# An encoder layer with a product-key expert FFN: chunk 0 routed before the last G, split weights for ten U blocks, one-hots moved to ScalarE, gathers spread later

## The chip, the cores and the metric

The kernel runs on one core of one Trainium2 chip. The metric is device time in microseconds, from one execution to the next of the same program; 0.5% of it is about 8 us. Five engines matter: TensorE (matmul, in the profile PE, its weight loads PEld), VectorE (DVE), ScalarE (ACT), GpSimd (POOL, here the queue of the gathers) and SyncE (SP, here the queue of all other loads and stores). Each works through its own list of instructions in order; semaphores tie the lists together.

## What is computed

One layer over 512 tokens of width 1024, in float32: two kinds of attention, a norm, and then the part that this case is about, a feed-forward layer with 16384 experts, each one row of a table U and one row of a table V. For each token, eight heads pick 16 experts each:

```python
q = (xb @ w_q).reshape(PEER_CHUNK, PEER_HEADS, PEER_KEY_DIM)
s1 = jnp.einsum('thd,kd->thk', q[..., :half], sub_keys[0])
s2 = jnp.einsum('thd,kd->thk', q[..., half:], sub_keys[1])
v1, i1 = lax.top_k(s1, PEER_TOPK)
v2, i2 = lax.top_k(s2, PEER_TOPK)
cand = (v1[..., :, None] + v2[..., None, :]).reshape(...)
cv, ci = lax.top_k(cand, PEER_TOPK)
...
idx = (e1 * PEER_N_KEYS + e2).reshape(PEER_CHUNK, PEER_HEADS * PEER_TOPK)
g = jax.nn.softmax(cv, axis=-1).reshape(PEER_CHUNK, -1)
hpre = jnp.einsum('td,ted->te', xb, u_table[idx])
act = g * jax.nn.gelu(hpre, approximate=False)
return jnp.einsum('te,ted->td', act, v_table[idx])
```

A gated term and the residual are added, and a last norm follows.

## The kernel before

The tokens are four chunks of 128. **Chunk 0 is gathered**: for each of its 128 slots, one indirect DMA fetches 128 rows of U (one per token, 512 KB), VectorE multiplies them with the tokens and sums; later the same with rows of V. **Chunks 1 to 3 are dense**: all 16384 experts are computed, in 128 blocks of 128. For the dense chunks the sparse weights g are spread into a matrix G (experts by tokens), which is written to DRAM and read back. The first 64 tokens of chunk 1 are mixed: their U products are gathered ("own rows", `own_rows`, 64 gathers of 128 rows, into the buffers `whi` and `wlo`), their V part is dense. So a U block covers N_U = 320 tokens, and an output block 384.

Matmuls at full precision are made of three at a reduced type: an operand is split into a high part (a cast on ScalarE, L78) and a low part (a subtraction on VectorE, L79), and `mm3` (L92 to L95) multiplies high x high, low x high, high x low. The `whole` form (L631) instead multiplies unsplit float32 weights with `whole`, a copy of the 320 tokens' h; it needs no cast, and each of its matmuls leaves two records in the trace. A matmul of the G step (L804), also float32, leaves two as well.

The work around the change, in order:

1. **Routing** (`route`, one call per chunk, four steps): VectorE alone, top-16 searches over candidate sums and lookups over 128 x 2048 tiles. For chunk 0 it ends in `i_sel`, the rows to gather.
2. **G** (`build_g`, one call per dense chunk): eight stages (each followed by a 1 MB store to `g_dram`), each of two steps of OT = 8 tokens. A step makes a first one-hot matrix for each token, `oh_i`: OV of the eight on VectorE in one instruction (L790), the others on ScalarE, one instruction each (L794), then one instruction over all of those (L795). VectorE makes the eight second ones (L799), TensorE multiplies eight pairs (L804), and ScalarE copies the result in two halves (L807) to the stage.
3. **Fill** (`filler`, advanced by `run_fill`): the gate product and then the first LEAD = 44 U blocks (`expert_in`), all in the whole form. A block is one 512 KB load, eight matmuls, one Gelu (L633). The Gelu of the first 16 blocks is stored in DRAM, of the others kept. `FILL_ROUTE` and `FILL_G` say how many fill steps are recorded per step of routing and stage of G, and `FILL_S` how many own rows.
4. The order is: routing of chunk 1; routing and G of chunk 2, then of chunk 3, with own rows and fill between; the G of chunk 1, whose weights include the own rows' results; routing of chunk 0; the rest of the fill. Then the memory of these stages (pool pR, which holds `whole` and the G buffers) is given up.
5. **The loop** over 128 blocks: as long as n + LEAD < 128 (84 turns) one more U block, in split form; then a V block is loaded and split, G is multiplied with the block's Gelu (L995), cast (`a_hi`) and subtracted (`a_lo`), and 18 output matmuls of 512 columns add into six accumulators. VectorE's order in the loop is written out by hand: each turn ends with some of the 257 gather steps of chunk 0 (L925 and L927 for U, L936 and L938 for V), which share four buffers `gat`. A turn with a U block counts 1, a later one 0.25, and the steps are spread evenly over that count:

```python
spent += 1 if n + LEAD < 128 else 0.25
upto = min(len(steps), math.ceil(len(steps) * spent / (128 - 0.75 * LEAD - 3)))
```

The loop's buffers lie where pool pR lay, so none of its loads can start before pR's tiles are done. Buffers named `raw` (three), `whi` and `wlo` (two each) serve all split weights before and in the loop, and psH two accumulators for U blocks. Outside the loop a scheduler sets the order within each engine from the order in which the steps were recorded.

Of the kernel before, what the change touches and what calls it, by code (L numbers as in the profile page):

```python
# [33 lines left out]
GB = 8  # L34
LEAD = 44
SPILL = 16
FILL_ROUTE = 1.7
FILL_G = 1.0
FILL_S = 2.8
OT = 8  # L40
OV = 5
NEG = -1e30
NA_KEYS = 256
NA_FROM = (0, 64, 192, 256)
# [10 lines left out]
def tile_encoder_layer(ctx: ExitStack, tc: tile.TileContext, A: dict, out: bass.AP):  # L55
# [550 lines left out]
    NGC, NDC = N_G // 128, N_D // 128  # L606
# [12 lines left out]
    def expert_in(i, whole=None):  # L619


        ps = psH.tile([128, 512], F32, name="hp")
        if whole is None:
            u = stream(A["uT"][i], [8, 128])
            for k in range(8):
                mm3(ps[:, :N_U], (u[0][:, k], u[1][:, k]), (hTh[:, k, ts], hTl[:, k, ts]), k == 0, k == 7)
        else:
            u = wst.tile([128, 8, 128], F32, name="raw", bufs=3)
            nc.sync.dma_start(u, A["uT"][i])
            for k in range(8):  # L630
                nc.tensor.matmul(ps[:, :N_U], u[:, k], whole[:, k, :], start=(k == 0), stop=(k == 7))  # L631
# [143 lines left out]
    def build_g(c, e1, e2, gw):  # L775
# [8 lines left out]
        for tg in range(128 // GT):  # L784
            stage = rt.tile([128, 128, GT], F32, name="g_st", bufs=2)
            for q in range(GT // OT):
# [5 lines left out]
                                        op=OP.is_equal)  # L792
                for i in range(OV, OT):
                    nc.scalar.activation(oi[:, i], iota, AF.Abs, bias=ne[:, t0 + i:t0 + i + 1])  # L794
# [22 lines left out]
    whole = rg.tile([128, 8, N_U], F32, name="whole")  # L817
# [25 lines left out]
    def filler():  # L843
        blocks = iter(range(LEAD))
        for hf in range(2):
            hs = slice(hf * 512, (hf + 1) * 512)
            gps = [ps_tile("mm", 4) for _ in range(4)]
            for kk in range(4):
                w = stream(A["gate_w"][kk * 256:(kk + 1) * 256, hs].rearrange("(k p) n -> p k n", p=128), [2, 512])
                for k2 in range(2):  # L850
                    k = 2 * kk + k2
                    for c in range(4):
                        cs = slice(c * 128, (c + 1) * 128)
                        mm3(gps[c], (hTh[:, k, cs], hTl[:, k, cs]), (w[0][:, k2], w[1][:, k2]), k == 0, k == 7)
                yield

            for c in range(4):
                pl = rg.tile([128, 512], F32, name="pl", bufs=2)
                nc.sync.dma_start(pl, ple_dram[c, :, hs])
                z = gps[c]  # L860
                nc.vector.tensor_tensor(z, z, gb[:, hs], op=OP.add)
                nc.scalar.activation(z, z, AF.Tanh, scale=0.5)
                nc.vector.scalar_tensor_tensor(z, z, 1.0, pl, op0=OP.add, op1=OP.mult)
                nc.vector.scalar_tensor_tensor(base[c][:, hs], h[c][:, hs], ALPHA, z, op0=OP.mult, op1=OP.add)
                if c % 2:
                    expert_in(next(blocks), whole)
                    yield
        for i in blocks:
            expert_in(i, whole)
            yield  # L870

    fill = filler()
    due = 2.0

    def run_fill(amount):
        nonlocal due
        due += amount
        while due >= 1:
            next(fill, None)
            due -= 1  # L880

    run_fill(0)
    gathers, g_due = iter(()), 0.0

    def run_own(amount):
        nonlocal g_due
        g_due += amount
        while g_due >= 1:
            next(gathers, None)
            g_due -= 1  # L890

    held = []
    for c in list(range(NGC, 4)):
        res = []
        for _ in route(c, res):
            run_fill(FILL_ROUTE)
            run_own(FILL_S)
        if c == NGC:
            held = res
            gathers = own_rows(*res)  # L900
            continue
        for _ in build_g(c, *res):
            run_fill(FILL_G)
            run_own(FILL_S)
    for _ in gathers:
        pass
    for _ in build_g(NGC, *held):
        run_fill(FILL_G)
    for c in range(NGC):
        for _ in route(c, []):  # L910
            run_fill(FILL_ROUTE)
    for _ in fill:
        pass
    pR.close()
# [52 lines left out]
    with tc.manual_schedule(engines={nc.vector.engine}):  # L967
        for n, i in enumerate(order):
            if n + LEAD < 128:
                expert_in(n + LEAD)  # L970
            if n % GB == 0:
                gt = gt_next
            if n % GB == GB // 2 and n + GB // 2 < 128:
                gt_next = load_g(n + GB // 2)
            raw = pE.tile([128, D], F32, name="v_raw", bufs=3)
            nc.sync.dma_start(raw, v_rows[i * 128:(i + 1) * 128, :])
            if n in (124, 125):
                vh = wst.tile([128, D], F32R, name="whi")
                vl = wst.tile([128, D], F32R, name="wlo")
                a2 = wst.tile([128, 2, N_D], F32R, name="raw", bufs=3)  # L980
                ah, al = a2[:, 0], a2[:, 1]
            else:
                vh = pE.tile([128, D], F32R, name="v_hi")
                vl = pE.tile([128, D], F32R, name="v_lo")
                ah = pE.tile([128, N_D], F32R, name="a_hi")
                al = pE.tile([128, N_D], F32R, name="a_lo")
            split(vh, vl, raw)
            if i < SPILL:
                ge = pE.tile([128, N_U], F32, name="ge_in", bufs=2)
                nc.sync.dma_start(ge, ge_dram[i])  # L990
# [121 lines left out]
```

## Time and profile before

| | |
|---|---|
| median of three runs | 1638.03 us (1636.96 to 1643.42) |
| the profiled execution | 1644.48 us, span 1642.7 us |
| TensorE busy | 1564.1 us, 95% of the span |
| VectorE busy | 1328.0 us, 81% |
| ScalarE busy | 671.3 us, 41% |
| GpSimd busy | 553.3 us, 34% |
| DMA | 409.13 MB, mean 249 GB/s |

The page of the profile shows shares of the whole span, groups of equal instructions with their mean time and with the idle time of the engine ahead of them, and the chain of waits from the end back to the start. Here the stages differ much, so they are read one by one: a table of busy time by stretch, then the timeline of single engines. In a timeline row stand start, length, engine, line, instruction, output and inputs, count, and in brackets the idle time ahead of it with what ended it. Line numbers are those of the kernel before.

### The profile page before, as it was taken

The numbers are of one execution on the slowest core, as the hardware profiler recorded it, in microseconds if no ns is written. First come the engines' busy times: TensorE is split into PE (matmuls) and PEld (weight loads), VectorE is DVE, ScalarE is ACT, GpSimd is POOL, SyncE is SP. The second block draws the span as 40 slices with busy tenths as digits, with TensorE's granted clock in tenths as the row PEclk, the third lists the DMA queues.
The fourth block names the chain that finished last, engine by engine and source line by source line (L and its number), as shares of the span: only waits on it lengthen the run. The fifth ranks groups of instructions, "written<-read, shape, count | busy, mean of one in ns | idle before, by whom it ended". The sixth has DMA issues, their size and how long they took to land.

```text
span 1642.7 us, 23609 instructions
## 1 busy us (share of the span) xinstructions
PE 1564.1 (95%) x8195; PEld 1309.7 (80%) x8195; DVE 1328.0 (81%) x2959; ACT 671.3 (41%) x1190; POOL 553.3 (34%) x407
## 2 busy tenths in 40 slices
PE   6999899999999999996899999999999999999997
PEld 4788677888777767784788888888898888888885
DVE  7366794699999999995778888878888888877776
ACT  3356684433324626682333333333343333333343
POOL 1013100000114453200455555555455565543200
PEclk9999999999999999998899999999999999999999
DMA  7242340332469988756899999999999999987763
GB/s 223 61 127 75 86 124 14 119 90 78 118 219 318 373 320 301 288 226 233 309 340 323 359 325 350 361 323 336 354 324 334 358 327 350 344 291 257 260 237 110
DMA packets 190583, 409.13 MB, mean 249 GB/s; under 512 B 14592, under 2 KB 100992, under 8 KB 187392
## 3 DMA queue, kind: packets, MB, share of 16 engines
q1 hardware_dynamic: 141696, 234.06, 41.9%
q0 software_dynamic: 48768, 173.56, 29.3%
q8 instruction: 65, 1.06, 0.3%
q14 instruction: 54, 0.44, 0.1%
HBM read 372.64 MB, written 31.98 MB: 246 GB/s over the span
## 4 chain that ended last, share of the span: by engine, by line
PE 40%; DMA 22%; issue 15%; DVE 14%; POOL 7%; ACT 2%; SPq 1%; DVEq 0%; POOLq 0%; ACTq 0%
DMA gat<-in_u_rows_dram,i_sel 11%; DMA gat<-in_v_rows_dram,i_sel 8%; PE hp L631 4%; PE acc L93 4%; PE acc L95 4%; PE acc L94 4%; POOL gat L925 3%; PE tr L804 3%; PE pj L93 3%; PE mm L93 3%; PE pj L94 3%; PE pj L95 3%; PE mm L94 3%; PE mm L95 3%; POOL gat L936 3%
## 5 line engine op out<-in xcount | busy, mean ns | idle before, releaser
L93 PE MATMUL acc<-v_hi,a_hi 128*128 128x512 f32 x756 | 297.6, 394 | 14.2 <-ACT a_hi L78 14.2
L95 PE MATMUL acc<-v_hi,a_lo 128*128 128x512 f32 x756 | 296.8, 393 | 0.0
L94 PE MATMUL acc<-v_lo,a_hi 128*128 128x512 f32 x756 | 294.9, 390 | 0.0
L925 POOL DMA_INDIRECT gat<-in_u_rows_dram,i_sel x128 | 203.2, 1588 | 260.2 <-DVE scr L927 147.8
L936 POOL DMA_INDIRECT gat<-in_v_rows_dram,i_sel x128 | 210.6, 1646 | 202.7 <-DVE base L938 172.6
L78 ACT CAST a_hi<-gt 128x384 fp32r<-128x384 f32 x126 | 64.9, 515 | 478.7 <-DVE gt L995 476.5
L95 PE MATMUL hp<-hTh,wlo 128*128 128x320 f32 x672 | 211.2, 314 | 17.9 <-DVE wlo L79 17.5
L93 PE MATMUL hp<-hTh,whi 128*128 128x320 f32 x672 | 208.7, 311 | 1.0 <-ACT ge L633 1.0
L94 PE MATMUL hp<-hTl,whi 128*128 128x320 f32 x672 | 208.2, 310 | 0.0
L631 PE MATMUL hp<-whole,raw 128*128 128x320 f32 x704 | 200.3, 433 | 0.0
L78 ACT CAST whi<-raw 128x1024 fp32r<-128x1024 f32 (+3 forms) x137 | 138.4, 1010 | 131.2 <-PE mm L94 53.1
L79 DVE TENSOR_TENSOR wlo<-raw,whi 128x1024 fp32r<-128x1024 f32 (+3 forms) x137 | 159.8, 1167 | 37.7 <-ACT whi L78 37.3
L79 DVE TENSOR_TENSOR v_lo<-v_raw,v_hi 128x1024 fp32r<-128x1024 f32 x126 | 153.7, 1220 | 39.4 <-DMA v_raw<-in_v_rows_dram 19.6
L927 DVE SCALAR_TENSOR_TENSOR scr<-gat,h 128x1024 f32<-128x1024 f32 x128 | 156.5, 1223 | 35.5 <-DMA gat<-in_u_rows_dram,i_sel 33.7
L938 DVE SCALAR_TENSOR_TENSOR base<-gat,hdot,base 128x1024 f32<-128x1024 f32 x128 | 164.1, 1282 | 21.6 <-DMA gat<-in_v_rows_dram,i_sel 20.1
L93 PEld LDWEIGHTS acc<-v_hi,a_hi 128*128 128x128 f32 x756 | 142.3, 188 | 41.9 <-ACT a_hi L78 15.4
L95 PEld LDWEIGHTS acc<-v_hi,a_lo 128*128 128x128 f32 x756 | 142.3, 188 | 33.7 <-DVE a_lo L79 1.4
L631 PEld LDWEIGHTS hp<-whole,raw 128*128 128x128 f32 x704 | 128.9, 190 | 45.6
L94 PEld LDWEIGHTS acc<-v_lo,a_hi 128*128 128x128 f32 x756 | 142.5, 188 | 27.6
L78 ACT CAST v_hi<-v_raw 128x1024 fp32r<-128x1024 f32 x126 | 131.9, 1047 | 54.6 <-PE acc L95 33.4
L95 PEld LDWEIGHTS hp<-hTh,wlo 128*128 128x128 f32 x672 | 127.3, 189 | 26.0 <-DVE wlo L79 25.9
L79 DVE TENSOR_TENSOR a_lo<-gt,a_hi 128x384 fp32r<-128x384 f32 x126 | 70.4, 559 | 80.4 <-ACT a_hi L78 79.1
(343 smaller groups left out, 2863.9 us busy)
## 6 DMA issues: line engine op xcount, KB each, us to landing
raw<-in_uT_dram SPq DMA_DIRECT2D x128, 512.0 KB
v_raw<-in_v_rows_dram SPq DMA_DIRECT2D x128, 512.0 KB
g_dram<-g_st SPq DMA_DIRECT2D x24, 1024.0 KB
gt<-g_dram SPq DMA_DIRECT2D x16, 1536.0 KB
raw<-in_w_in_dram SPq DMA_DIRECT2D x17, 512.0 KB
raw<-in_w_q_dram SPq DMA_DIRECT2D x16, 512.0 KB
na_b<-in_na_bias_dram POOLq DMA_DIRECT2D x32, 128.0 KB
raw<-in_w_o_dram SPq DMA_DIRECT2D x8, 512.0 KB
```

Source lines behind the costliest of these rows:

```text
L78: nc.scalar.copy(hi, src)
L79: nc.vector.tensor_tensor(lo, src, r32(hi), op=OP.subtract)
L93: nc.tensor.matmul(ps, a[0], b[0], start=start, stop=False)
L94: nc.tensor.matmul(ps, a[0], b[1], start=False, stop=False)
L95: nc.tensor.matmul(ps, a[1], b[0], start=False, stop=stop)
L631: nc.tensor.matmul(ps[:, :N_U], u[:, k], whole[:, k, :], start=(k == 0), stop=(k == 7))
L804: nc.tensor.matmul(ps[:, i * 128:(i + 1) * 128], oj[:, 4 * r + i, :], oi[:, 4 * r + i, :], start=True, stop=True)
L925: nc.gpsimd.indirect_dma_start(out=u[:], out_offset=None, in_=u_rows, in_offset=bass.IndirectOffsetOnAxis(ap=i_sel[:, c, k:k + 1], axis=0))
L927: nc.vector.scalar_tensor_tensor(scr, u, 1.0, h[c], op0=OP.mult, op1=OP.mult, accum_out=hdot[:, c, k:k + 1])
L936: nc.gpsimd.indirect_dma_start(out=u[:], out_offset=None, in_=v_rows, in_offset=bass.IndirectOffsetOnAxis(ap=i_sel[:, c, k:k + 1], axis=0))
L938: nc.vector.scalar_tensor_tensor(base[c], u, hdot[:, c, k:k + 1], base[c], op0=OP.mult, op1=OP.add)
```

## The change

Six numbers and the order of the stages change. The numbers of instructions that differ are: 80 fewer `whole` matmuls (ten blocks), 240 more split ones, ten more casts each on ScalarE and VectorE, 144 more L794, L795 over 768 elements instead of 384, and L790 over 256 instead of 640. GpSimd's list is the same.

```diff
-FILL_ROUTE = 1.7
-FILL_G = 1.0
-FILL_S = 2.8
+SPLIT_LEAD = 10
+FILL_ROUTE = 1.3
+FILL_G = 0.35
+FILL_OWN = 0.7
+OWN = 2.8
+LATE_GATHER = 0.4
 OT = 8
-OV = 5
+OV = 2
...
         for i in blocks:
-            expert_in(i, whole)
+            expert_in(i, whole if i < LEAD - SPLIT_LEAD else None)
             yield
...
-    held = []
-    for c in list(range(NGC, 4)):
-        res = []
-        for _ in route(c, res):
-            run_fill(FILL_ROUTE)
-            run_own(FILL_S)
-        if c == NGC:
-            held = res
-            gathers = own_rows(*res)
-            continue
-        for _ in build_g(c, *res):
-            run_fill(FILL_G)
-            run_own(FILL_S)
-    for _ in gathers:
+    def paced(steps, rate, own=None):
+
+        due = 0.0
+        for _ in steps:
+            due += OWN if own is not None else 0
+            while due >= 1:
+                next(own, None)
+                due -= 1
+            run_fill(rate + (FILL_OWN if own is not None else 0))
+
+    held = []
+    paced(route(NGC, held), FILL_ROUTE)
+    own = own_rows(*held)
+    for c in range(NGC + 1, 4):
+        res = []
+        paced(route(c, res), FILL_ROUTE, own)
+        paced(build_g(c, *res), FILL_G, own)
+    for _ in own:
         pass
-    for _ in build_g(NGC, *held):
-        run_fill(FILL_G)
     for c in range(NGC):
-        for _ in route(c, []):
-            run_fill(FILL_ROUTE)
+        paced(route(c, []), FILL_ROUTE)
+    paced(build_g(NGC, *held), FILL_G)
     for _ in fill:
         pass
...
-            spent += 1 if n + LEAD < 128 else 0.25
-            upto = min(len(steps), math.ceil(len(steps) * spent / (128 - 0.75 * LEAD - 3)))
+            spent += 1 if n + LEAD < 128 else LATE_GATHER
+            upto = min(len(steps), math.ceil(len(steps) * spent / (128 - (1 - LATE_GATHER) * LEAD - 3)))
```

So chunk 0's routing comes before the G of chunk 1 instead of after it; the last ten of the 44 U blocks done ahead no longer read `whole`; two of eight first one-hots stay on VectorE; fewer fill steps are recorded beside a stage of G without own rows, and about as many as before beside one with them (0.35 + 0.7); and a turn of the loop without a U block counts 0.4 in the spread of the gathers.

More of the change, by code (lines that the diff above doesn't have):

```diff
@@ L882, in tile_encoder_layer @@
     run_fill(0)
[L883 to L890, printed above, removed]
+    def paced(steps, rate, own=None):
[6 more added lines that the diff above has]
+            run_fill(rate + (FILL_OWN if own is not None else 0))
     held = []
-    for c in list(range(NGC, 4)):
+    paced(route(NGC, held), FILL_ROUTE)
+    own = own_rows(*held)
+    for c in range(NGC + 1, 4):
         res = []
-        for _ in route(c, res):
-            run_fill(FILL_ROUTE)
-            run_own(FILL_S)
-        if c == NGC:
-            held = res
-            gathers = own_rows(*res)
-            continue
-        for _ in build_g(c, *res):
-            run_fill(FILL_G)
-            run_own(FILL_S)
-    for _ in gathers:
-        pass
-    for _ in build_g(NGC, *held):
-        run_fill(FILL_G)
+        paced(route(c, res), FILL_ROUTE, own)
+        paced(build_g(c, *res), FILL_G, own)
+    for _ in own:
+        pass
     for c in range(NGC):
-        for _ in route(c, []):
-            run_fill(FILL_ROUTE)
+        paced(route(c, []), FILL_ROUTE)
+    paced(build_g(NGC, *held), FILL_G)
     for _ in fill:
```

## The prediction

> **What bounds the kernel now.** I read the table by stage first, because the share of the whole span (TensorE 95%) averages stages with different limits. The stages are cut where the trace changes: routing and the G of chunks 2 and 3 (440 to 690), the G of chunk 1 (690 to 737), routing of chunk 0 (737 to 762), a hole, the loop with U blocks (782 to 1451) and the loop without (to 1622). Columns: stage, length, then busy us and instructions of TensorE, weight loads, VectorE, ScalarE, GpSimd; granted clock, DMA share, GB/s.
>
> ```profile
> 440.00:690.00 250.00, 240.77 (x1182) 183.91 (x1181) 242.84 (x648) 110.59 (x247) 93.21 (x64) 1.00 0.82 297
> 512.00:586.00 74.00, 73.03 (x411) 58.01 (x411) 72.49 (x200) 44.44 (x107) 30.30 (x23) 1.00 0.94 346
> 622.00:690.00 68.00, 67.00 (x385) 53.83 (x384) 66.89 (x185) 43.23 (x106) 21.61 (x16) 1.00 0.84 307
> 690.00:737.00 47.00, 47.00 (x325) 40.90 (x324) 46.97 (x162) 40.73 (x101) 0.00 (x0) 1.00 0.58 223
> 737.00:762.00 25.00, 25.00 (x95) 17.64 (x95) 22.96 (x79) 6.89 (x11) 0.00 (x0) 1.00 0.44 159
> 762.00:782.00 20.00, 4.79 (x31) 4.19 (x29) 1.66 (x3) 5.09 (x7) 3.78 (x4) 0.68 0.85 304
> 782.00:1451.00 669.00, 651.12 (x3499) 579.39 (x3500) 557.18 (x698) 227.63 (x331) 376.61 (x234) 0.99 0.95 338
> 1451.00:1622.00 171.00, 170.94 (x749) 139.10 (x748) 124.39 (x163) 69.44 (x90) 33.47 (x19) 1.00 0.71 247
> ```
>
> Up to 737 VectorE is never free (242.84 of 250, 46.97 of 47). ScalarE is half idle while chunks 2 and 3 get their G, but not in the G of chunk 1: 40.73 of 47. From 762 to 782 nearly everything stands still, and the clock falls to 0.68. The next rows (timeline: start, length, instruction, idle before it and its releaser) show that hole and TensorE's pace around it.
>
> ```profile
> 736.94 25.47 PE L631 MATMUL hp<-whole,raw 128*128 128x320 f32 x94
> 762.48 0.38 SPq L962 DMA_DIRECT2D gt<-g_dram  x1
> 779.76 1.23 DVE L79 TENSOR_TENSOR v_lo<-v_raw,v_hi 128x1024 fp32r<-128x1024 f32 x1 [19.56 <-DMA v_raw<-in_v_rows_dram]
> 781.99 0.79 PE L93 MATMUL acc<-v_hi,a_hi 128*128 128x512 f32 x1 [14.17 <-ACT a_hi L78]
> 788.13 0.31 PE L95 MATMUL hp<-hTh,wlo 128*128 128x320 f32 x1
> 791.36 0.40 PE L93 MATMUL acc<-v_hi,a_hi 128*128 128x512 f32 x1
> 795.26 0.39 PE L95 MATMUL acc<-v_hi,a_lo 128*128 128x512 f32 x1
> ```
>
> The first loads of the loop leave only at 762.48, when the last whole-weight block, and with it the memory of the G stage, is done. VectorE then waits 19.56 us for a V block. A whole block costs 25.47 / 94 x 16 = 4.34 us of TensorE (16 records each). Split matmuls follow each other at (791.36 - 788.13) / 22 = 0.147 us, so a split block of 24 takes 3.52; an output matmul takes (795.26 - 791.36) / 17 = 0.229, 18 of them 4.13. A turn of the loop with a U block is thus 7.65 us of TensorE, but 84 turns took 669, 7.96 each. VectorE's groups in 782 to 1451 say why (last columns: idle ahead of the group, and what ended it), and so do four starts of the same instruction in successive turns:
>
> ```profile
> L927 DVE SCALAR_TENSOR_TENSOR scr<-gat,h 128x1024 f32<-128x1024 f32 x128 | 156.5, 1223 | 35.5 <-DMA gat<-in_u_rows_dram,i_sel 33.7
> L938 DVE SCALAR_TENSOR_TENSOR base<-gat,hdot,base 128x1024 f32<-128x1024 f32 x106 | 136.0, 1283 | 21.6 <-DMA gat<-in_v_rows_dram,i_sel 20.1
> L79 DVE TENSOR_TENSOR a_lo<-gt,a_hi 128x384 fp32r<-128x384 f32 x84 | 46.9, 559 | 54.6 <-ACT a_hi L78 53.3 <-issue 1.3
> 1001.43 0.56 DVE L79 TENSOR_TENSOR a_lo<-gt,a_hi 128x384 fp32r<-128x384 f32 x1 [0.64 <-ACT a_hi L78]
> 1008.98 0.56 DVE L79 TENSOR_TENSOR a_lo<-gt,a_hi 128x384 fp32r<-128x384 f32 x1 [0.64 <-ACT a_hi L78]
> 1017.18 0.56 DVE L79 TENSOR_TENSOR a_lo<-gt,a_hi 128x384 fp32r<-128x384 f32 x1 [0.64 <-ACT a_hi L78]
> 1023.46 0.56 DVE L79 TENSOR_TENSOR a_lo<-gt,a_hi 128x384 fp32r<-128x384 f32 x1 [0.64 <-ACT a_hi L78]
> ```
>
> A turn with three gathers keeps VectorE 7.55 us (1001.43 to 1008.98) if no gather is late, one with two 6.28 (1017.18 to 1023.46). 257 steps over 92 units are 2.79 a turn, 7.28 us; the waits for gathers, 33.7 + 20.1 = 53.8 us, add 0.64: 7.92. So VectorE, in its written order, sets the turn, and late gathers push it past TensorE.
>
> **The loop with fewer gathers a turn.** The new spread divides by 128 - 0.6 x 44 - 3 = 98.6: 2.61 steps a turn, in the order 3, 3, 2, 3, 2. VectorE's own work is then (3 x 7.55 + 2 x 6.28) / 5 = 7.04. Even with the old wait of 0.64 it asks for 7.68, about TensorE's 7.65. DMA does not forbid it: 338 GB/s over 7.96 us is 2.69 MB a turn, less 0.18 of a 0.52 MB gather is 2.60, at 338 GB/s 7.69 us. But 651.12 us of busy TensorE over 84 turns is 7.75, and I take that: 84 x (7.96 - 7.75) = -18 us. Ends: -27 (7.65) and -8 (7.87, half of the waits stay).
>
> The gathers put off go to the 44 later turns, 1.04 a turn instead of 0.7. There a gather in each turn makes VectorE's chain as long as the output matmuls:
>
> ```profile
> 1504.14 0.56 DVE L79 TENSOR_TENSOR a_lo<-gt,a_hi 128x384 fp32r<-128x384 f32 x1 [0.64 <-ACT a_hi L78]
> 1508.50 0.56 DVE L79 TENSOR_TENSOR a_lo<-gt,a_hi 128x384 fp32r<-128x384 f32 x1 [0.92 <-ACT a_hi L78]
> ```
>
> This pair is 4.36 us apart, TensorE's turn 4.13. Over 36 turns that is at most 36 x 0.23 = 8 us, at least nothing; most of it hides behind the two buffers ahead of TensorE, so +3. The last gather comes four turns later, some eight turns before the end, and the norm of chunk 0 still fits there.
>
> **Six of eight one-hots on ScalarE.** Groups in 690 to 737, the G of chunk 1, of 16 steps of eight tokens; then one step on each engine; then a wide cast, for the price of width.
>
> ```profile
> L807 ACT COPY g_st<-tr 128x512 f32<-128x512 f32 x32 | 18.7, 583 | 5.5 <-PE tr L804 5.4
> L794 ACT ACTIVATE oh_i<-iota,ne 128x128 f32<-128x128 f32 x48 | 15.9, 397 | 0.0
> L795 ACT ACTIVATE oh_i<-oh_i 128x384 f32<-128x384 f32 x16 | 8.4, 526 | 0.2
> L790 DVE TENSOR_TENSOR oh_i<-iota,eT 128x640 f32<-128x640 f32 x16 | 12.9, 808 | 0.0
> 697.47 0.81 DVE L790 TENSOR_TENSOR oh_i<-iota,eT 128x640 f32<-128x640 f32 x1
> 700.25 0.81 DVE L790 TENSOR_TENSOR oh_i<-iota,eT 128x640 f32<-128x640 f32 x1
> 704.65 1.95 PE L804 MATMUL tr<-oh_i,oh_j 128*128 128x128 f32 x16
> 705.28 0.53 ACT L795 ACTIVATE oh_i<-oh_i 128x384 f32<-128x384 f32 x1
> 705.74 0.59 ACT L807 COPY g_st<-tr 128x512 f32<-128x512 f32 x1
> 706.63 0.59 ACT L807 COPY g_st<-tr 128x512 f32<-128x512 f32 x1 [0.31 <-PE tr L804]
> L78 ACT CAST v_hi<-v_raw 128x1024 fp32r<-128x1024 f32 x126 | 131.9, 1047 | 54.6 <-PE acc L95 33.4
> ```
>
> A step is 2.78 us of VectorE now (697.47 to 700.25). 256 elements instead of 640 cut it by 0.40 to 0.48 (0.808 x 384 / 640 at most; some of an instruction does not scale). ScalarE's step grows: three more L794 at 15.9 / 48 = 0.33 are 1.0; L795 over 768 lies between 526 and 1047 ns, 0.84, 0.31 more. Its 40.73 / 16 = 2.55 becomes 3.8 if it never waits. In its written order (three L794, copy, one, copy, two, L795) each first copy also waits for half of the eight matmuls that L795 released, 1 us of the 1.95 above, while three L794 cover only 0.9 of that and of the hand-overs: 0.3 to 0.4 a step, as in the row at 706.63. I take 4.1 us, ScalarE now setting the pace. The G of chunk 1 goes from 46 to 16 x 4.1 + 1 = 67: +21. Ends: 3.6 (the rows' starts are closer than their lengths, 0.46 of 0.53) gives +13, 4.4 gives +25.
>
> For chunks 2 and 3, where own rows are dotted between the steps, a step is 74 / 16 = 4.6 and 68 / 16 = 4.25 us. VectorE falls by 0.4 to 4.1 and 3.8, ScalarE rises by 1.3 to 4.1 and 4.0 before any wait, and DMA is at 0.94 and 0.84. Three limits lie within 0.5 us, so I take 0. Ends: -13 (32 x 0.4, all of VectorE's cut is gained) and +10 (0.3 a step lost to ScalarE's order).
>
> **The reordered stage and the split weights.** In the built programs 34.5 whole blocks stand ahead of chunk 1's G before; after it is 30 ahead of chunk 0's routing. In that routing come four whole and three split blocks, 4 x 4.34 + 3 x 3.52 = 28 us of TensorE, beside 23 us of routing and 5 casts of 1.2 on VectorE: also 28. The fifth cast waits for a buffer that the third split block frees, and chunk 1's one-hots stand behind it on VectorE, and behind that block's Gelu on ScalarE, so they start after all 28. Two split blocks fit into the G, and 142 matmuls x 0.147 = 21 us follow it; the last G store, the G load and V blocks run under them. The hole took 19.5 us from load to first output matmul, a store now comes first, so I add 2: 23. SP's stores of that G stand behind the eighth split load, which waits only for the fifth cast; GpSimd's order does not change. Sum from 690: 28 + 67 + 23 = 118 us against 92 (690 to 782), +26, of which +21 is the line above and +5 this. If the loads were not covered, the hole would be 20 again: ends +3 and +15.
>
> **Sum:** +5 (order) + 21 (G of chunk 1) + 0 (G of chunks 2, 3) - 18 (loop) + 3 (late turns) = +11. The profiled execution took 1644.48 us (span 1642.7), 6.4 above the median of the three runs, so 1655.5 in its own terms is 1649 against 1638.03.
>
> **The rivals.**
> *ScalarE doesn't set the pace (faster).* If its step is 3.6, since its rows overlap, the G of chunk 1 costs +13, and chunks 2 and 3 follow VectorE, -13. Then +5 + 13 - 13 - 18 + 3 = -10: 1628. It decides from a step under about 3.9. For it: VectorE is at 98% in 440 to 690, ScalarE at 44%. Against it: 40.73 of 47 already, and DMA at 0.94.
> *The parts cancel.* The loop falls to 7.65, all 54 us of waits hidden: -27, and +5 + 21 + 0 - 27 + 3 = +2: 1640. For it: 2.61 steps ask VectorE for only 7.04. Against it: 7.75 of TensorE is busy in a turn.
> *TensorE cools in the G of chunk 1.* It works 1.95 us and waits 2.1, sixteen times. If the clock is halved there, as it nearly was in the hole (0.68), its 1.95 becomes 3.9, both copies wait longer, and a step is about 5.8: 16 x 1.7 = +27 more, 1676. Against it: the clock fell only where TensorE stood for 14 us. The Trainium skill, "TensorE: Matmul & The Clock Gate", section "A second HAM failure mode: psum-queue depth-cycling", speaks for it: frequent short idling between groups of matmuls makes the clock swing between half and full; no run here shows it yet.
>
> **How the numbers follow.** Forecast 0.45 (its own range 1640 to 1662), ScalarE not the limit 0.27, cancelling 0.20, cooling 0.08. The measurement can tell 0.5%, 8 us, from no change. The forecast is slower by more than that in most of its range, and some of it reaches into the middle: slower 0.50, same 0.21, faster 0.29. The range takes in the faster case with a larger gain in the loop and most of the cooling: 1621 to 1671.
>
> **What would show it.** Right: in chunk 1's G ScalarE is busy all the time and steps are 4 us apart, TensorE idle for half of it; no wait of 10 us or more ahead of the first output matmul, and no fall of the clock there; the loop's turns 7.7 to 7.8 us, with waits for gathers well under 50 us; later turns 4.1 to 4.2. Wrong: steps of chunk 1's G under 3.8, the G of chunks 2 and 3 shorter than 74 and 68, a turn still at 7.9, or a hole ahead of the first output matmul.

## The result, and the profile after

| | before | after |
|---|---|---|
| median | 1640.65 us (10 runs) | 1652.82 us (10 runs) |
| ratio, 95% interval | | 1.0068 (1.0045 to 1.0091) |
| profiled execution: span | 1642.7 us | 1650.8 us |
| loop's first `a_lo` | 781.97 us | 806.41 us |
| 84 turns with a U block | 669.3 us | 638.7 us |
| later turns, to the last `a_lo` seen | 170.6 us | 185.2 us |
| from there to the end of the span | 20.9 us | 20.5 us |

The kernel became slower by 0.7%. The loop starts 24.4 us later, its turns with a U block take 30.6 us less, the turns behind them 14.7 more, the tail 0.4 less: +8.1 us, the difference of the two spans. (The medians differ by 12.2; the profiled execution of the kernel before lay 3.8 above its median, that of the changed kernel 0.2 below.)

The table by stage of the changed kernel follows, columns as in the prediction. Its stages are routing and G of chunks 2 and 3, routing of chunk 0, the G of chunk 1, what lies between it and the loop, the loop, the later turns.

```profile
440.00:690.00 250.00, 229.71 (x1120) 177.75 (x1119) 233.84 (x683) 142.60 (x341) 79.29 (x64) 0.95 0.79 289
690.00:717.00 27.00, 26.47 (x133) 21.61 (x132) 24.43 (x62) 8.45 (x14) 0.00 (x0) 1.00 0.48 175
717.00:780.00 63.00, 42.72 (x313) 39.58 (x311) 43.52 (x148) 61.39 (x151) 0.00 (x0) 0.97 0.34 141
780.00:806.00 26.00, 20.79 (x141) 20.53 (x140) 6.53 (x6) 8.35 (x13) 3.97 (x4) 0.96 0.93 325
806.00:1445.00 639.00, 637.39 (x3486) 573.95 (x3487) 537.23 (x682) 235.74 (x335) 351.50 (x218) 1.00 0.96 342
1445.00:1630.00 185.00, 177.98 (x764) 142.39 (x763) 142.69 (x178) 68.40 (x90) 55.60 (x34) 0.99 0.78 271
```

In the G of chunk 1 ScalarE is busy 61.39 of 63 us, TensorE only 42.72: the engines changed places, as forecast. Up to 690 TensorE lost 11 us of work (229.71 against 240.77), and its granted clock there is 0.95 for 1.00: it stands for 5.26 us from 453 us on and for 6.17 us from 622 us on, and the clock is 0.60 from 455 to 460 us and 0.67 from 625 to 630. In the loop TensorE is now busy 637.39 of 639: it is the bound there, and VectorE is not.

First TensorE, then ScalarE in two steps of chunk 1's G (timelines), then ScalarE's groups in 717 to 780:

```profile
743.35 2.10 PE L807 MATMUL tr<-oh_i,oh_j 128*128 128x128 f32 x16 [1.79 <-ACT oh_i L798]
746.96 2.10 PE L807 MATMUL tr<-oh_i,oh_j 128*128 128x128 f32 x16 [1.50 <-ACT oh_i L798]
```

```profile
742.47 0.83 ACT L798 ACTIVATE oh_i<-oh_i 128x768 f32<-128x768 f32 x1
743.21 0.97 ACT L797 ACTIVATE oh_i<-iota,ne 128x128 f32<-128x128 f32 x3
744.10 0.58 ACT L810 COPY g_st<-tr 128x512 f32<-128x512 f32 x1
744.58 0.40 ACT L797 ACTIVATE oh_i<-iota,ne 128x128 f32<-128x128 f32 x1
745.00 0.58 ACT L810 COPY g_st<-tr 128x512 f32<-128x512 f32 x1
745.48 0.69 ACT L797 ACTIVATE oh_i<-iota,ne 128x128 f32<-128x128 f32 x2
746.07 0.83 ACT L798 ACTIVATE oh_i<-oh_i 128x768 f32<-128x768 f32 x1
```

```profile
L797 ACT ACTIVATE oh_i<-iota,ne 128x128 f32<-128x128 f32 x96 | 32.8, 394 | 0.0
L810 ACT COPY g_st<-tr 128x512 f32<-128x512 f32 x32 | 18.7, 585 | 1.6 <-PE tr L807 1.5
L798 ACT ACTIVATE oh_i<-oh_i 128x768 f32<-128x768 f32 x16 | 13.4, 835 | 0.0
L81 ACT CAST whi<-raw 128x1024 fp32r<-128x1024 f32 x3 | 3.1, 1037 | 2.1 <-PE hp L97 2.1
L636 ACT ACTIVATE ge<-hp 128x320 f32<-128x320 f32 x3 | 1.3, 428 | 0.0
```

A step is 746.07 - 742.47 = 3.60 us, and ScalarE never waits in it: its instructions start closer together than they are long (0.74 us for the 0.83 of L798). The two copies of a step, which I had let wait for TensorE, wait 1.6 us in all 16 steps together. What the estimate left out is at the bottom of the groups: the casts and Gelus of the split blocks, 3.1 + 1.3 = 4.4 us. 16 x 3.60 + 4.4 = 62.0, nearly the 62.8 us from the G's first transpose to its last matmul (716.84 to 779.6).

Next, VectorE's groups in 806 to 1445, and from its timeline the loop's first `a_lo`, the first late one, and three intervals of late turns:

```profile
L923 DVE SCALAR_TENSOR_TENSOR scr<-gat,h 128x1024 f32<-128x1024 f32 x128 | 156.5, 1222 | 28.6 <-DMA gat<-in_u_rows_dram,i_sel 26.7
L934 DVE SCALAR_TENSOR_TENSOR base<-gat,hdot,base 128x1024 f32<-128x1024 f32 x90 | 115.4, 1282 | 14.1 <-DMA gat<-in_v_rows_dram,i_sel 12.6
```

```profile
806.41 0.56 DVE L82 TENSOR_TENSOR a_lo<-gt,a_hi 128x384 fp32r<-128x384 f32 x1 [0.58 <-ACT a_hi L81]
1445.08 0.56 DVE L82 TENSOR_TENSOR a_lo<-gt,a_hi 128x384 fp32r<-128x384 f32 x1 [0.63 <-ACT a_hi L81]
...
1453.01 0.56 DVE L82 TENSOR_TENSOR a_lo<-gt,a_hi 128x384 fp32r<-128x384 f32 x1 [0.92 <-ACT a_hi L81]
1453.48 2.60 DVE L934 SCALAR_TENSOR_TENSOR base<-gat,hdot,base 128x1024 f32<-128x1024 f32 x2
1458.25 0.56 DVE L82 TENSOR_TENSOR a_lo<-gt,a_hi 128x384 fp32r<-128x384 f32 x1 [0.63 <-ACT a_hi L81]
...
1470.15 0.56 DVE L82 TENSOR_TENSOR a_lo<-gt,a_hi 128x384 fp32r<-128x384 f32 x1 [0.64 <-ACT a_hi L81]
...
1474.23 0.56 DVE L82 TENSOR_TENSOR a_lo<-gt,a_hi 128x384 fp32r<-128x384 f32 x1 [0.63 <-ACT a_hi L81]
...
1478.76 1.23 DVE L82 TENSOR_TENSOR v_lo<-v_raw,v_hi 128x1024 fp32r<-128x1024 f32 x1 [2.77 <-ACT v_hi L81]
...
1481.02 0.56 DVE L82 TENSOR_TENSOR a_lo<-gt,a_hi 128x384 fp32r<-128x384 f32 x1 [0.63 <-ACT a_hi L81]
```

(1445.08 - 806.41) / 84 = 7.60 us a turn; the waits for gathers fell from 53.8 to 39.3 us. A late turn with one gather takes 4.08 us (1470.15 to 1474.23), TensorE's own pace, one with two 5.24 (1453.01 to 1458.25), and the one at 1474.23 takes 6.79, because ScalarE's cast came late. ScalarE's timeline says what that cast waited for, and SP's what stood ahead of it in the queue:

```profile
1477.68 1.05 ACT L81 CAST v_hi<-v_raw 128x1024 fp32r<-128x1024 f32 x1 [3.48 <-DMA v_raw<-in_v_rows_dram]
```

```profile
1457.24 4.25 SPq L972 DMA_DIRECT2D v_raw<-in_v_rows_dram  x2
1462.76 0.38 SPq L958 DMA_DIRECT2D gt<-g_dram  x1
1465.10 19.17 SPq L972 DMA_DIRECT2D v_raw<-in_v_rows_dram  x5
```

The V block that is late was asked for after a 1.5 MB load of G rows. Such waits recur about every eight turns, as the G loads do.

### The profile page after: what moved, and what is told of

It is laid out like the page before. It is cut to its first block, busy times and chain, and to the rows that moved or that the text cites. A ratio compares the mean times of both kernels' runs of the same rounds, so it can differ in the third digit from the quotient of the medians.

```text
span 1650.8 us, 23986 instructions
## 1 busy us (share of the span) xinstructions
PE 1560.6 (95%) x8275; PEld 1321.2 (80%) x8275; DVE 1321.0 (80%) x2969; ACT 735.7 (45%) x1344; POOL 536.7 (33%) x407
## 4 chain that ended last, share of the span: by engine, by line
PE 68%; DVE 14%; DMA 7%; ACT 5%; issue 5%; POOL 1%; SPq 0%; ACTq 0%; DVEq 0%; POOLq 0%
PE acc L96 9%; PE acc L98 9%; PE acc L97 9%; PE hp L96 6%; PE hp L98 6%; PE hp L97 6%; PE pj L96 3%; PE mm L97 3%; PE mm L96 3%; PE mm L98 3%; PE pj L97 3%; PE pj L98 3%; DVE oh_j L802 3%; DMA v_raw<-in_v_rows_dram 2%; DMA wlo<-in_u_rows_dram,s_sel 2%
## 5 line engine op out<-in xcount | busy, mean ns | idle before, releaser
L96 PE MATMUL acc<-v_hi,a_hi 128*128 128x512 f32 x756 | 299.0, 396 | 12.7 <-ACT a_hi L81 12.6
L932 POOL DMA_INDIRECT gat<-in_v_rows_dram,i_sel x128 | 203.2, 1587 | 217.6 <-DVE base L934 192.4
L96 PE MATMUL hp<-hTh,whi 128*128 128x320 f32 x752 | 232.5, 309 | 1.4 <-ACT whi L81 1.4
L98 PE MATMUL hp<-hTh,wlo 128*128 128x320 f32 x752 | 231.7, 308 | 1.7 <-DVE wlo L82 1.7
L97 PE MATMUL hp<-hTl,whi 128*128 128x320 f32 x752 | 231.8, 308 | 0.0
L81 ACT CAST whi<-raw 128x1024 fp32r<-128x1024 f32 (+3 forms) x147 | 148.6, 1011 | 156.6 <-PE mm L97 52.8
L82 DVE TENSOR_TENSOR wlo<-raw,whi 128x1024 fp32r<-128x1024 f32 (+3 forms) x147 | 172.1, 1171 | 53.9 <-ACT whi L81 53.4
L923 DVE SCALAR_TENSOR_TENSOR scr<-gat,h 128x1024 f32<-128x1024 f32 x128 | 156.5, 1222 | 28.6 <-DMA gat<-in_u_rows_dram,i_sel 26.7
L934 DVE SCALAR_TENSOR_TENSOR base<-gat,hdot,base 128x1024 f32<-128x1024 f32 x128 | 164.0, 1281 | 14.2 <-DMA gat<-in_v_rows_dram,i_sel 12.6
L634 PE MATMUL hp<-whole,raw 128*128 128x320 f32 x544 | 156.2, 436 | 0.0
L96 PEld LDWEIGHTS hp<-hTh,whi 128*128 128x128 f32 x752 | 141.2, 188 | 4.9 <-ACT whi L81 1.6
L97 PEld LDWEIGHTS hp<-hTl,whi 128*128 128x128 f32 x752 | 141.1, 188 | 3.3
L98 PEld LDWEIGHTS hp<-hTh,wlo 128*128 128x128 f32 x752 | 141.6, 188 | 2.5 <-DVE wlo L82 2.5
```

The lines of the kernel that those rows point to most:

```text
L81: nc.scalar.copy(hi, src)
L82: nc.vector.tensor_tensor(lo, src, r32(hi), op=OP.subtract)
L96: nc.tensor.matmul(ps, a[0], b[0], start=start, stop=False)
L97: nc.tensor.matmul(ps, a[0], b[1], start=False, stop=False)
L98: nc.tensor.matmul(ps, a[1], b[0], start=False, stop=stop)
L923: nc.vector.scalar_tensor_tensor(scr, u, 1.0, h[c], op0=OP.mult, op1=OP.mult, accum_out=hdot[:, c, k:k + 1])
```

## The experiments

All twelve ran beside the kernel before, and ratios are against it; its own median lay between 1640.7 and 1647.0 us in them, so ratios compare better than medians. The stages are read from the `a_lo` rows, as in the table above; the last column is TensorE's busy time in the 390 us from 440 to 830, when the fixed work ahead of the loop is done. The lower it is, the more TensorE stood. The stages are from one execution each. Five kernels have the same program ahead of the loop (before, e4, e5, e6, e10), and start it at 780.7 to 784.9: differences of up to 4 us in that column say nothing.

| run | median us | ratio (95%) | loop starts | with U | later | TensorE 440-830 |
|---|---|---|---|---|---|---|
| before | | 1 | 782.0 | 669.3 | 170.6 | 362.0 |
| after | 1652.8 | 1.0068 (1.0045-1.0091) | 806.4 | 638.7 | 185.2 | 342.1 |
| e1 order, split | 1655.9 | 1.0063 (1.0037-1.0089) | 792.9 | 669.1 | 172.2 | 355.5 |
| e2 OV 5 | 1638.3 | 0.9963 (0.9946-0.9981) | 795.1 | 639.5 | 181.1 | 353.6 |
| e3 spread 0.25 | 1668.5 | 1.0146 (1.0122-1.0171) | 808.3 | 665.2 | 170.4 | 340.5 |
| e4 before, spread 0.4 | 1626.6 | 0.9888 (0.9866-0.9909) | 784.9 | 638.7 | 181.0 | 363.1 |
| e5 e4, G loads in quarters | 1619.9 | 0.9845 (0.9819-0.9870) | 782.6 | 636.5 | 176.9 | 365.2 |
| e6 e4, 4 V buffers | 1623.7 | 0.9857 (0.9833-0.9882) | 782.6 | 637.6 | 182.3 | 365.4 |
| e7 e2, all whole | 1640.4 | 0.9970 (0.9954-0.9986) | 795.8 | 638.8 | 188.5 | 355.1 |
| e8 before, OV 2 | 1656.0 | 1.0061 (1.0040-1.0082) | 792.2 | 663.9 | 171.1 | 354.9 |
| e9 e2, fill 1.7 | 1653.2 | 1.0040 (1.0023-1.0056) | 809.4 | 640.4 | 184.4 | 341.7 |
| e10 e5, more buffers | 1619.1 | 0.9839 (0.9813-0.9865) | 780.7 | 637.6 | 175.2 | 364.9 |
| e11 e5, OV 2 in chunks 2, 3 | 1629.0 | 0.9903 (0.9879-0.9926) | 791.1 | 635.8 | 176.5 | 358.1 |
| e12 e4, two stages swapped | 1636.5 | 0.9943 (0.9922-0.9965) | 791.2 | 639.1 | 180.8 | 359.9 |

**e1, the order and the split blocks alone.**

```diff
-LATE_GATHER = 0.4
+LATE_GATHER = 0.25
 OT = 8
-OV = 2
+OV = 5
```

> The changed order of the stages and the ten split blocks alone: OV is 5 again and LATE_GATHER 0.25. Theory, from the two traces: the new order costs about 10 us by itself (first output matmul 118.2 us after the end of chunk 3's G in the changed kernel, 91.3 before, so +26.9, of which the G of chunk 1 has 16.8), the G of chunk 1 is back at 46 us, the loop turns at 7.96 and the late ones at 4.08: 1651 us, 10 over the kernel before. Rival, the order costs only through the longer G that it puts last: 1641, no difference. Second rival, the split blocks themselves shorten the loop, as its first loads come earlier relative to it: under 1640.

The loop starts 10.9 us later than before and then runs as before: the theory.

**e2, the one-hots undone.**

```diff
-OV = 2
+OV = 5
```

> The changed kernel with OV back at 5 (three of eight first one-hots on ScalarE instead of six), all else as changed. Theory, ScalarE sets the pace of chunk 1's G: its 16 steps fall from 3.7 to 2.8 or 2.9 us, the stage from 62.8 to about 46, the G of chunks 2 and 3 grow by 2 or 3 us in sum: 1638 to 1640 against 1653, and first output matmul 14 us earlier. Rival, the G of chunk 1 is long because two split blocks (their casts and subtractions, and their Gelus) and SP's queue share it: the stage stays above 58 us and the time at 1650 or more.

The loop starts 11.3 us earlier than in the changed kernel, and the time is 0.9963 of before: ScalarE's share of the one-hots had turned a gain into a loss. From e3 to e1 the same edit is worth 15.4 us of the loop's start.

**e3 and e4, the spread: undone, and done alone.** In e3:

```diff
-LATE_GATHER = 0.4
+LATE_GATHER = 0.25
```

> The changed kernel with LATE_GATHER back at 0.25, all else as changed. Theory, the gathers that are put off give the loop its 30.6 us and cost the late turns 14.7: turns with a U block go from 7.60 back to 7.96 us, later ones from 4.43 to 4.08 with 0.7 gathers each, 1653 + 16 = 1669. Rival, the loop got faster because it starts with more loads ahead (or with a later start that lets the gathers run ahead), and the spread only cost the late turns: turns stay below 7.75 and the time is 1638 to 1645.

In e4 on the kernel before:

```diff
-            spent += 1 if n + LEAD < 128 else 0.25
-            upto = min(len(steps), math.ceil(len(steps) * spent / (128 - 0.75 * LEAD - 3)))
+            spent += 1 if n + LEAD < 128 else 0.4
+            upto = min(len(steps), math.ceil(len(steps) * spent / (128 - 0.6 * LEAD - 3)))
```

> The kernel before with nothing but the later spread of the gathers (0.25 becomes 0.4, 0.75 becomes 0.6). Theory, the spread is worth the same without the rest: -30.6 in the turns with a U block, +14.7 in the later ones, 1641 - 16 = 1625. Rival, it is worth something only behind a loop that starts without the stop of TensorE ahead of it: 1637 or more.

Both came out as the theory has it. The spread alone gives 1.1%, 30.6 us in the loop against 10.4 lost in the later turns; it is the whole gain of the change, and it does not need the rest.

**e5 and e6, the cause of the late turns' loss.** e5, built on e4, cuts each G load in four by groups of tokens (`load_g`, not shown, takes a part):

```diff
...
-            if n % GB == GB // 2 and n + GB // 2 < 128:
-                gt_next = load_g(n + GB // 2)
+            part = n % GB - 3
+            if 0 <= part < 4 and n - n % GB + GB < 128:
+                gt_next = load_g(n - n % GB + GB, gt_next if part else None, part)
```

> The kernel of e4 (before, with the later spread alone, 1626.6 us) with each 1.5 MB load of G rows cut into four quarters that are issued with four successive turns instead of one. Theory, the late turns lose their time to bursts of DMA: after each G load a V block comes late, in e4 four times, with 2.46, 2.83, 1.36 and 0.48 us of VectorE's waits and 2.31 for one load of stored Gelu rows: the late turns fall from 4.46 us to 4.15 to 4.25, 181 us to about 172, and the time to 1617 to 1620. Rival, it is the gathers on VectorE (turns with two of them take 5.24 us instead of 4.08, turns with one have no slack) or the mean DMA rate: the late turns stay at 4.4 and the time at 1625 to 1630.

e6, on e4 too, gives V blocks one more buffer instead:

```diff
-            raw = pE.tile([128, D], F32, name="v_raw", bufs=3)
+            raw = pE.tile([128, D], F32, name="v_raw", bufs=4)
```

> The kernel of e4 with a fourth buffer for V blocks, loads of G rows whole as before. Theory of bursts: a V block is then asked for one turn earlier, 4.1 us in the late turns, more than the longest wait seen (3.5 us on ScalarE): waits for V blocks go, late turns 4.15 to 4.25, 1617 to 1621. Rival (VectorE's gathers or the mean rate): no change, 1625 to 1630.

e5's time is the one that the theory gave, but only 4.1 of the 6.7 us lie in the later turns, 176.9 us where 172 were forecast; the rest lies ahead of them, within what kernels with the same program there differ by. The 4 us recur: with quartered loads the later turns take 175.2 to 176.9 us (e5, e10, e11), with whole loads and the same spread 180.8 to 188.5 (the changed kernel, e2, e4, e6, e7, e9, e12). Rows of VectorE's timeline of e5:

```profile
1480.67 0.56 DVE L79 TENSOR_TENSOR a_lo<-gt,a_hi 128x384 fp32r<-128x384 f32 x1 [0.64 <-ACT a_hi L78]
1481.15 1.28 DVE L938 SCALAR_TENSOR_TENSOR base<-gat,hdot,base 128x1024 f32<-128x1024 f32 x1
1482.49 1.23 DVE L79 TENSOR_TENSOR v_lo<-v_raw,v_hi 128x1024 fp32r<-128x1024 f32 x1
1483.63 0.48 DVE L998 TENSOR_TENSOR gt<-gt,ge 128x320 f32<-128x320 f32 x1
1484.75 0.56 DVE L79 TENSOR_TENSOR a_lo<-gt,a_hi 128x384 fp32r<-128x384 f32 x1 [0.64 <-ACT a_hi L78]
```

Between 1432 and 1546 us no V block is late, and turns with one gather take 4.08 us: VectorE has room for a gather in each. What stays are two turns with two gathers, one long wait for a V block at the start (3.63 us) and some of 0.4 to 1.0 near the end. In e6 the waits for V blocks after G loads go too up to 1550, but then one load of stored Gelu rows costs 3.86 us and a V block 2.67, and the later turns as a whole are no shorter: an earlier request moved the waits, smaller loads removed some. (The ratios of e5 and e6 can't be told apart.)

**e7, whole blocks in the new order.**

```diff
-SPLIT_LEAD = 10
+SPLIT_LEAD = 0
...
-OV = 2
+OV = 5
```

> The kernel of e2 (changed, OV = 5, 1638 us) with SPLIT_LEAD = 0: all 44 blocks done ahead in the whole form, the order of the stages as changed. Theory, the split blocks are what keeps the new order from costing more: the loop's first loads wait for the last whole block, some 20 us of whole blocks follow the G and then the 14 us stop of TensorE comes back: 15 to 20 us more than e2, 1653 to 1658. Rival, the loads wait for the last store of the G rather than for the whole blocks, and whole blocks cover as well as split ones: 1638 to 1645.

My theory fell. The loop starts at 795.8, with the split blocks at 795.1, and the times can't be told apart. The rows of TensorE's timeline of e7 at the end of chunk 1's G show what happened:

```profile
756.42 1.95 PE L807 MATMUL tr<-oh_i,oh_j 128*128 128x128 f32 x16
758.21 1.24 PE L634 MATMUL hp<-whole,raw 128*128 128x320 f32 x4
759.29 1.95 PE L807 MATMUL tr<-oh_i,oh_j 128*128 128x128 f32 x16
761.07 13.62 PE L634 MATMUL hp<-whole,raw 128*128 128x320 f32 x50
...
795.80 0.80 PE L96 MATMUL acc<-v_hi,a_hi 128*128 128x512 f32 x1 [15.69 <-ACT a_hi L81]
```

The stop of 15.7 us does come back, but chunk 1's G is over at 761 instead of 768.8: whole blocks need nothing from ScalarE or VectorE but a Gelu and fill the 1 us that TensorE has free in each step, and split ones, which need a cast and a subtraction from the two engines beside it, don't. From its first to its last matmul that G takes 44.1 us, TensorE standing for 0.1; in e2 it takes 48.0, TensorE standing for 6.2 and VectorE never. It also starts 3.7 us earlier. What split blocks cover behind the G they cost ahead of it.

**e8, the one-hots alone.**

```diff
-OV = 5
+OV = 2
```

> The kernel before with OV = 2 alone: six of eight first one-hots on ScalarE, everything else as before. Theory, ScalarE's work of 3.6 to 3.7 us a step sets the pace of chunk 1's G also without split blocks beside it: 46 becomes 58 to 60 us, the G of chunks 2 and 3 lose 2 or 3 us: +10 to +12 against the kernel before, 0.6 to 0.8% slower. Rival, the 62.8 us of the changed kernel were mostly the casts and Gelus of split blocks on ScalarE: the step is 3.2 or less, the stage at most 52, and with what chunks 2 and 3 gain the time is that of before within 4 us.

0.6% slower, the theory's figure; its loop starts 10.2 us later, without any split block. But the parts are not the theory's. The G of chunk 3 ends 7.3 us earlier than before (683.4), and the G of chunk 1 then takes 65.5 us, not 58 to 60. Busy times in that stage:

```profile
683.40:749.00 65.60, 64.11 (x386) 52.64 (x385) 61.83 (x237) 62.22 (x157) 0.00 (x0) 1.00 0.51 193
```

TensorE (64.11) is as tight there as ScalarE (62.22), since the routing of chunk 0 and more U blocks than before now lie beside this G. So e8 shows what the one-hots cost, but not that ScalarE alone sets the pace in the old order; in the changed kernel, where TensorE stands for a third of the stage, it does.

**e9, FILL_ROUTE at its old value.**

```diff
-FILL_ROUTE = 1.3
+FILL_ROUTE = 1.7
...
-OV = 2
+OV = 5
```

> The kernel of e2 (changed, OV = 5, 1638 us) with FILL_ROUTE at 1.7, as it was before the change, instead of 1.3. Theory: the new order costs 11 us because fewer U blocks are placed beside the first routing; TensorE spends 145 us on U blocks between 440 and 690 in e1, e2 and e7, 156 before, and has to do the missing 10 us after 690, where it has no free time. With 1.7 it spends about 155 again, the loop's last U turn comes 8 to 10 us earlier and the time is 1628 to 1631. Rival: the loop cannot start earlier, since after the last G its loads share DMA at 0.95 to 0.98 with the split blocks' loads and the last stores; blocks done earlier only leave TensorE idle there, and the time stays at 1636 to 1641.

Both sides were wrong: 15 us slower than e2. TensorE is busier in the first routing, as the theory had it (68.1 of 72 us in 440 to 512, 60.2 in e2), but the G of chunk 3 ends at 707.4 instead of 693.6, which is nearly all of the loss. TensorE's timeline from the end of the G of chunk 2:

```profile
590.49 45.38 PE L634 MATMUL hp<-whole,raw 128*128 128x320 f32 x168
...
648.32 3.75 PE L807 MATMUL tr<-oh_i,oh_j 128*128 128x128 f32 x16 [8.35 <-DVE oh_j L802]
```

The delay is there before that G begins: its first matmul starts at 648.3, in e2 at 626.7, and from there it is done sooner than in e2 (59.1 us, 67.1 in e2). Beside own rows FILL_OWN comes on top, so a step of routing has 1.7 + 0.7 = 2.4 fill steps, not the old 1.7 (e2: 2.0): 182 records of whole blocks stand between the two G's, 140 in e2, and then TensorE waits 8.35 us for VectorE. So e9 doesn't say what the old rate would do in the new order (e12 does), and that the fuller routing is the whole cause was read from the trace, not tried.

**e10, more buffers on top of e5.**

```diff
-name="v_raw", bufs=3
+name="v_raw", bufs=4
...
-name="ge_in", bufs=2
+name="ge_in", bufs=3
```

> The kernel of e5 (before, later spread, G loads in quarters, 1620 us) with a fourth V buffer and a third one for stored Gelu rows as well. Theory of bursts: the waits that are left in e5's late turns (3.63 us for one V block at the first of them, 0.4 to 1.0 for five loads near the end) shrink, 3 to 5 us: 1615 to 1617. Rival: what is left is DMA's mean rate, so that a load asked for earlier only takes its time from another: 1619 to 1622.

1619.1 against 1619.9: no difference that this measurement shows, the rival's case.

**e11, six one-hots on ScalarE only where it is half idle.**

```diff
+OV_MORE = 2
...
+        ov = OV if c == NGC else OV_MORE
```

> The kernel of e5 with two of eight first one-hots on VectorE (OV = 2) in the G of chunks 2 and 3 alone, and five, as before, in the G of chunk 1. Theory: beside own rows VectorE is the limit and ScalarE half idle, so there the move gains: the G of chunk 3 ended at 683.4 instead of 690.7 us in e8. 5 to 7 us less than e5: 1613 to 1615. Rival: DMA, at 0.94 beside the G of chunk 2, or ScalarE's written order takes it back, as in the changed kernel (688.3 instead of 690.7): 1617 to 1621.

Neither: 9 us slower than e5. The G of chunk 3 did end at 683.3 as expected. The U blocks' share of TensorE's time in 440 to 690 of e5, then of e11, and the last rows of whole blocks in the same order, say where that went:

```profile
440.00:690.00 250.00, 155.17 (x550) 101.45 (x551) 0.00 (x0) 14.76 (x34) 1.00 0.82 297
```

```profile
440.00:690.00 250.00, 143.54 (x502) 91.76 (x502) 0.00 (x0) 13.45 (x31) 1.00 0.83 295
```

```profile
737.53 25.47 PE L631 MATMUL hp<-whole,raw 128*128 128x320 f32 x94
```

```profile
741.81 30.31 PE L632 MATMUL hp<-whole,raw 128*128 128x320 f32 x112
```

TensorE did 11.6 us less of the U blocks by 690, since fewer of its records fit between the steps, and did them later: the G of chunk 1 takes 58.5 us instead of 46.3, TensorE busy nearly throughout, and whole blocks end at 772.1 instead of 763.0. TensorE has a fixed amount of work ahead of the loop; a G that ends earlier while TensorE stands (233.17 busy of 250, in e5 240.49) only moves the work back.

**e12, the two stages swapped, at the old fill rates.**

```diff
-SPLIT_LEAD = 10
-FILL_ROUTE = 1.3
-FILL_G = 0.35
-FILL_OWN = 0.7
+SPLIT_LEAD = 0
+FILL_ROUTE = 1.7
+FILL_G = 1.0
+FILL_OWN = 0.0
...
-OV = 2
+OV = 5
```

> The changed kernel with OV = 5, SPLIT_LEAD = 0 and the fill rates of the kernel before (1.7 a step of routing, 1.0 a stage of G, none beside own rows): of the change only the order (chunk 0 routed before the G of chunk 1) and the later spread are left, so it is e4 (1626.6 us) with the two stages swapped. It tells apart what the 11 us are that e1, e2 and e7 lose against the kernels with the old order. Theory, they lie in the fill rates: TensorE is the limit of the whole stretch from 440 us to the loop, and it was idle 28 us of 440 to 830 before, 27 in e4, but 34.5, 36.4 and 34.9 in e1, e2 and e7: with the old rates it is idle 27 to 29 us and the time is 1626 to 1631. Rival, the order itself costs them: a G that stands last leaves only its own gaps for blocks and then its last store ahead of the loop's loads: idle 33 us or more, 1636 to 1641.

The time lies at the rival's figure, TensorE's standing time (30.1) between the two. The loop starts at 791.2: 6.3 us after e4, 4.6 before e7, which differs from it in the fill rates alone. The order has a part: by ratio e12 is 0.55% behind e4, clear of noise. The part of the fill rates is not shown: the ratios of e12 and e7 overlap (0.9922-0.9965 and 0.9954-0.9986). Two of SP's rows of the kernel before, and three of e12, show one place where the swap costs:

```profile
458.93 14.05 SPq L629 DMA_DIRECT2D raw<-in_uT_dram  x3
473.03 1.11 SPq L826 DMA_DIRECT2D s_sel<-s_ix  x2
```

```profile
459.04 0.33 SPq L632 DMA_DIRECT2D raw<-in_uT_dram  x1
464.73 1.11 SPq L829 DMA_DIRECT2D s_sel<-s_ix  x2
472.21 0.34 SPq L632 DMA_DIRECT2D raw<-in_uT_dram  x1
```

The rewritten pacing records own rows ahead of the fill, so that the copies of their indices stand in SP's queue ahead of two U loads; TensorE is busy 64.1 of the 72 us from 440 to 512 there, at a clock of 0.94; before, 68.0 at 1.00. The other place is the end: the last G store leaves at 769.92, the loop's G load at 773.97, and TensorE then stands 16.57 us (e4: 13.68). That these two make up the 6.3 us was read from the traces, not tried.

The fastest versions that ran are e5 and e10, the later spread alone with smaller G loads: 0.9845 and 0.9839 of the time before (e6, at 0.9857, can't be told from them). The other parts of the change did not pay in any combination tried.

## Why the prediction was right, and where its terms were not

The sign and the size came out: +11 forecast, +12.2 measured between the medians. That the size came out is luck. The loop's term missed by 12.6 us one way and the later turns' by 11.7 the other, both outside their own ranges; order (5 us too low) and the G of chunk 1 (4 us too high) cancel too. By its own signs the step of that G, 3.60 us, spoke against the forecast ("under 3.8"). What was right, and tried, is that ScalarE's new share lengthens the last G, that the order costs and that the spread of the gathers shortens the loop. Term by term, from the two profiled executions, whose spans differ by 8.1:

| term | forecast | in the traces | tried by |
|---|---|---|---|
| order, between the G's | +5 (+3 to +15) | +10.1 | e1: +10.9, e12 |
| G of chunk 1 | +21 (+13 to +25) | +16.8 (62.8 us for 46) | e2, e3, e8 |
| G of chunks 2 and 3 | 0 (-13 to +10) | -2.5 (688.2 for 690.7) | e8, e11 |
| loop with U blocks | -18 (-27 to -8) | -30.6 | e3, e4 |
| later turns | +3 (0 to +8) | +14.7 | e4, e5, e6 |

*Order.* Routing of chunk 0 beside seven blocks was put at 28 us and took 28.6 (688.25 to 716.84). Behind the G 23 were forecast and 26.8 came (779.6 to 806.43). The stop of TensorE was indeed covered by split blocks but for 5.65 us; "I add 2" for a store was too little. That the split blocks cover it at no cost was wrong (e7).

*G of chunk 1.* The mechanism holds: ScalarE sets the pace, TensorE waits 1.5 to 1.8 us in nearly every step. The size was 3.60 for 4.1, since ScalarE's instructions overlap by 0.07 to 0.1 us each and the waits that I added per copy don't occur (my own sum, 2.55 + 1.0 + 0.31, is 3.86 before any wait, not 3.8); 4.4 us of the split blocks' casts and Gelus, which I had left out, put some of it back. The rival with a step of 3.6 had the right step and the wrong conclusion: at 3.6 ScalarE still is the slowest engine.

*G of chunks 2 and 3.* "All of VectorE's cut is gained" was the lower end. e11 shows that an earlier end there is no gain at all: TensorE, at 240.77 of 250, is as tight as VectorE (242.84, 97%; I wrote 98), and the U blocks it then misses are done after 690. I read VectorE as the bound of that stage and TensorE's column beside it as mere activity.

*Loop.* The step that failed is "651.12 us of busy TensorE over 84 turns is 7.75, and I take that". Busy time is no floor. The records overlap: an output matmul is 0.39 us long and has its successor 0.227 behind, so the last one ahead of a stop counts with 0.16 us more, about 4 us for the 27 stops of that stage (an estimate); and the loop's first nine were at half clock (0.63 to 0.79 us long, granted clock 0.50 from 782 to 786), some 2 us more. The rest of the 13 us between 651.12 and 84 x 7.60 was not placed. Nor was 7.65 a floor, whose 0.229 us an output matmul was read just after the stop. The later turns of the same trace, 28 of them from 1451.25 on, take 4.08 us each on average with 18 output matmuls, 3.52 + 4.08 = 7.60, and that is what the turn became. VectorE's own 7.04 and its waits of 0.47 fit under it.

*Later turns.* "A gather in each turn makes VectorE's chain as long as the output matmuls" failed: the pair of rows 4.36 us apart was an exception, and e5 holds 4.08 with a gather in each turn. What the gathers took is DMA: with 271 GB/s instead of 247 in these turns, the burst of a G load is no longer absorbed, and a V block or stored Gelu rows come late. Of the 10.4 us that the spread costs there (e4), smaller loads removed 4; a wait of 3.6 us for the first V block stayed, and why is open, since neither a fourth buffer (e6) nor more of both kinds (e10) shortened these turns beyond doubt. Turns with two gathers (5.24 for 4.08) add about a microsecond each, twice.

*TensorE cooling in the G.* It did not cool for most of it: the first row below, of the changed kernel, has the clock at 1.00 through 50 us of chunk 1's G, with idle times of 1.5 to 1.8 us in every step from 734 us on. But the argument against this rival, that the clock fell only where TensorE stood for 14 us, misread the trace before: there it is also 0.65 from 174 to 178 us, around the end of a stop of 2.46 us. In the changed kernel it is 0.66 from 550 to 555 us, behind a stop of 1.80, and 0.50 from 778 to 780, behind stops of 1.50 and 1.41. So a short stop is followed by a fall at times, and mostly not; what decides it, these runs don't show.

```profile
720.00:770.00 50.00, 32.92 (x252) 30.66 (x253) 36.01 (x133) 49.89 (x127) 0.00 (x0) 1.00 0.33 137
770.00:780.00 10.00, 6.91 (x42) 6.25 (x41) 4.92 (x11) 8.54 (x18) 0.00 (x0) 0.84 0.40 156
800.00:810.00 10.00, 4.35 (x14) 3.34 (x13) 5.14 (x8) 5.17 (x7) 1.61 (x1) 0.71 1.02 382
```

The Trainium skill, "TensorE: Matmul & The Clock Gate", section "A second HAM failure mode: psum-queue depth-cycling", has frequent short idling make the clock swing; in those 50 us this trace does not agree. In the next ten it may: the clock falls to 0.84 although TensorE's longest idle time there is 1.5 us. The same page's section "What's actually happening" puts the fall after an idle window of about 3.4 us, and the 1.00 in the steps and the 0.71 around the stop of 5.65 us agree with that, the 0.84 and the falls behind 1.80 and 2.46 us do not.

## What to carry to other kernels

Here two engines were both above 95% of a stage, and making one of them faster gained nothing (e11), as the other's work neither shrank nor moved into real idle time: count TensorE's standing time up to a fixed point, not the end of the stage that was sped up. Take an engine's floor from a stretch where it alone sets the pace, not from its busy time in a stage with stalls. And when transfers are put off into a stage that seemed free, look at the bursts of that stage, not at its mean rate: smaller loads gained where earlier ones moved the wait.

## What was not expected of the hardware

Records of neighbouring ScalarE instructions overlap: 128 columns take 0.39 us by their record, three of them 0.97 together, and 768 columns 0.83, with the next one 0.74 behind. So six small instructions and the wide one cost a step 3.60 - 2 x 0.48 = 2.64 us, while the sum of their records is 6 x 0.39 + 0.84 = 3.2.

TensorE held the full clock for 40 us (734 to 774) in steps of some 3.6 us of which it idles 1.5 to 1.8, and lost it elsewhere behind a single stop of 1.80 us (0.66 from 550 to 555). An output matmul of 512 columns has its successor 0.227 us behind (4.08 / 18).
